# Attention order with two units under way, and a readout with stationary values in column halves

## The chip, the cores and the metric

The kernel runs on one core of one Trainium2 chip. The metric is the device time of one execution in microseconds (us), median over several runs. A core has TensorE (PE, matrix products into PSUM banks), VectorE (DVE), ScalarE (ACT), GpSimd (POOL) and SyncE (SP, which issues most of the DMAs). Each engine works through its own instructions in the order in which the program lists them, and waits where an operand isn't ready or a buffer isn't free.

## The reference

Two layers over 256 tokens of width 1024: a gated DeltaNet, then sparse attention (NSA) with 16 heads of 64 in 4 groups of keys and values, each with a DeepNorm residual and a layer norm. The change lies in the second layer:

```python
proj = x @ w_in                       # q (1024), z (3 x 1024), gate logits (48)
q = rope(q); gates = sigmoid(logits)
p_cmp = masked_softmax(q @ k_cmp.T * scale)   # 15 compressed blocks
p_sel = masked_softmax(q @ k_sel.T * scale)   # all 256 tokens: 4 blocks of 64, top 16
p_win = masked_softmax(q @ k_win.T * scale)   # a window of 512 covers all
o = sum over branches of gates * (p @ v) * silu(z)
y = o @ w_out
x = layer_norm(alpha * x + y)
```

## The kernel before

Tokens lie in two tiles of 128 (t = 0, 1). Projections run as products of three fp32r matmuls (high and low parts of both operands, L233 to L235). Weights stream through a ring of five raw buffers; ACT casts the high part (L181), POOL subtracts the low part (L185). The work of projections is cut into pieces of six matmuls of 512 columns, kept in a list: `fill(n)` puts the next n pieces into PE's order, and runs what was deferred (`step`).

Attention is cut into 24 units. A unit of the first tile holds two heads (keys of the first tile alone), a unit of the second tile one head; a pair of them is read out together. The string `UNITS` gives the order of tiles, `FA` and `FB` the number of fills at two places of each turn of the loop. The steps of a unit:

- `scores` (L1318): four fp32r matmuls into one of two PSUM score buffers.
- `maxima`: DVE adds the mask and takes the negated maxima, for the second tile L1331 to L1334.
- `exps` (L1347, L1348 or L1351, L1352): ACT, into SBUF tiles `pt` (both token branches) and `Pc` (the compressed one).
- `transposes`: PE turns `pt` into the PSUM buffer "t", of which there is one (`ptp`, L1360), and `Pc` (L1362).
- `probs`: ACT copies them to `PT` (L1367) and `PcT` (L1371).
- `readout` (L1386 or L1389, L1392): the turned probabilities are stationary, the values with a 65th column of ones move, into the one PSUM buffer "o". The column of ones gives the denominators.
- `total` (L1400 to L1404), deferred by a step: DVE multiplies by gates, reciprocal denominators and `zz` (silu of z, made at L1218 and L1219), and sums the branches.
- `merge`: four or two column blocks of the sum are turned on PE into buffer "t" (`tp_b`, L1418); ACT makes the high part `x1h` (L1422), DVE the low part `x1l` (L1423), from which the out projection (`pbo` and `pbl`) is computed. There are two merges for the first tile, four for the second.

Behind the out projection stand the residual and layer norm: L905, L906, L912 on DVE, L913 and L914 on POOL, then for the first tile L941 on DVE, L945 on ACT and two products on POOL. In the second half of the out projection the second tile's pieces are 12 matmuls of 256 columns.

Fills of the z projection run out at about 338 us; from there on the pieces are those of the out projection, which need the merges. The main loop computes the scores of unit i first, then copies, fills, reads out unit i-1, and transposes unit i at the end of the same turn.

## Time and profile before

| | us |
|---|---|
| median of 3 runs | 393.89 (393.65 to 393.94) |
| the profiled execution | 393.75 |
| its span | 391.9 |
| PE busy in the span | 379.6 (97%) |
| DVE, ACT, POOL busy | 223.6, 220.6, 246.3 |
| PE busy in the attention stage, 240.9 to 384 | 142.22 of 143.10 |

The span runs from the first instruction to the last; 1.85 us of the profiled execution's time lie outside it. In a timeline a row begins with its start and length in us; matmuls are pipelined, so the spacing of starts tells their pace better than their lengths. An fp32 matmul or transposition leaves one or two records, of which "x8" counts the records. Where an engine was idle before a row, brackets give how long and what ended it.

### The profile page before, as it was taken

To read this page: it belongs to the slowest core of one execution; us is meant where nothing else is said; L and a number is where in the kernel's file an instruction comes from. 1 tells how busy PE (TensorE), PEld (TensorE's weight loads), DVE (VectorE), ACT (ScalarE), POOL (GpSimd) and SP (SyncE) were. 2 spreads that over 40 slices of the span, in tenths; PEclk is the share of its full clock that TensorE was granted. 3 is DMA by queue.
4 is the path that set the end of the run, shared out by engine and by line. 5 is a ranking of instruction groups with operands and counts; after the bars stand their busy time and mean duration, and the time that the engine had idled before them with its cause. 6 is when DMAs were issued, how large, how long until landed. Compare 5 with 4: busy or idle time off the path is not lost.

```text
span 391.9 us, 7551 instructions
## 1 busy us (share of the span) xinstructions
PE 379.6 (97%) x2870; PEld 335.5 (86%) x2870; DVE 223.6 (57%) x591; ACT 220.6 (56%) x433; POOL 246.3 (63%) x154
## 2 busy tenths in 40 slices
PE   8999999999999999999999999999999999999991
PEld 6999999999989987877998788888888888878891
DVE  2868776668623445463641755545656465676726
ACT  4688666656663462625563649566474747456410
POOL 5699999747444846894764988193544637209051
PEclk9999999999999999999999999999999999999997
DMA  7876578654334315573736764243415243301011
GB/s 226 324 223 221 206 232 291 190 135 164 110 110 138 125 35 186 163 248 125 204 118 214 278 223 150 103 153 115 164 39 175 64 153 109 107 3 54 3 54 54
DMA packets 23476, 58.68 MB, mean 150 GB/s; under 512 B 6672, under 2 KB 9232, under 8 KB 23312
## 3 DMA queue, kind: packets, MB, share of 16 engines
q1 hardware_dynamic: 23232, 58.13, 44.9%
q8 instruction: 22, 0.36, 0.4%
q14 instruction: 14, 0.11, 0.1%
q10 hardware_dynamic: 144, 0.07, 0.1%
q0 software_dynamic: 64, 0.01, 0.0%
HBM read 55.96 MB, written 2.23 MB: 148 GB/s over the span
## 4 chain that ended last, share of the span: by engine, by line
PE 42%; DVE 4%; ACT 3%; DMA 2%; POOL 2%; issue 1%; POOLq 0%; DVEq 0%; SPq 0%; ACTq 0%
PE pbz L233 6%; PE pbz L234 6%; PE pbz L235 6%; PE op L1389 4%; PE s L1318 3%; PE ptp L1360 3%; PE op L1392 2%; PE op L1386 1%; DMA raw_bz<-in_bz 1%; ACT hi_bq L181 1%; POOL lo_bq L185 1%; PE pskv L235 1%; PE pbo L233 1%; PE pskv L233 1%; PE pskv L234 1%; PE qtp L1205 1%
## 5 line engine op out<-in xcount | busy, mean ns | idle before, releaser
L185 POOL TENSOR_TENSOR lo_bz<-raw_bz,hi_bz 128x1024 fp32r<-128x1024 f32 x24 | 56.8, 2387 | 39.3 <-ACT hi_bz L181 21.7
L185 POOL TENSOR_TENSOR lo_wqkv<-raw_wqkv,hi_wqkv 128x1024 fp32r<-128x1024 f32 x22 | 52.6, 2408 | 6.7 <-ACT hi_wqkv L181 4.5
L233 PE MATMUL pbz<-hi_bz,x1h 128*128 128x512 f32 x96 | 38.9, 405 | 0.0
L234 PE MATMUL pbz<-hi_bz,x1l 128*128 128x512 f32 x96 | 37.7, 393 | 0.0
L235 PE MATMUL pbz<-lo_bz,x1h 128*128 128x512 f32 x96 | 37.6, 392 | 0.0
L185 POOL TENSOR_TENSOR lo_bo<-raw_bo,hi_bo 128x1024 fp32r<-128x1024 f32 x8 | 18.9, 2390 | 22.8 <-ACT hi_bo L181 17.7
L185 POOL TENSOR_TENSOR lo_skv<-raw_skv,hi_skv 128x1024 fp32r<-128x1024 f32 x12 | 28.4, 2399 | 5.0 <-PE pskv L235 5.0
L185 POOL TENSOR_TENSOR lo_wz<-raw_wz,hi_wz 128x1024 fp32r<-128x1024 f32 x8 | 19.4, 2440 | 16.9 <-ACT hi_wz L181 16.8
L1367 ACT COPY PT<-ptp 128x512 f32<-128x512 f32 x24 | 14.1, 588 | 24.0 <-PE ptp L1360 24.0
L181 ACT CAST hi_bz<-raw_bz 128x1024 fp32r<-128x1024 f32 x24 | 25.2, 1052 | 2.9 <-DMA raw_bz<-in_bz 1.6
L185 POOL TENSOR_TENSOR lo_wo<-raw_wo,hi_wo 128x1024 fp32r<-128x1024 f32 x8 | 18.9, 2385 | 11.5 <-ACT hi_wo L181 11.5
L185 POOL TENSOR_TENSOR lo_bq<-raw_bq,hi_bq 128x1024 fp32r<-128x1024 f32 x8 | 19.1, 2394 | 10.8 <-ACT hi_bq L181 10.8
L181 ACT CAST hi_wqkv<-raw_wqkv 128x1024 fp32r<-128x1024 f32 x22 | 22.7, 1043 | 1.0 <-DMA raw_wqkv<-in_wqkv 1.0
L233 PEld LDWEIGHTS pbz<-hi_bz,x1h 128*128 128x128 f32 x96 | 18.0, 188 | 4.1
L235 PEld LDWEIGHTS pbz<-lo_bz,x1h 128*128 128x128 f32 x96 | 18.0, 188 | 4.1
L234 PEld LDWEIGHTS pbz<-hi_bz,x1l 128*128 128x128 f32 x96 | 18.0, 188 | 2.7
L1351 ACT ACTIVATE pt<-s,mx 128x256 f32<-128x256 f32 x32 | 13.4, 472 | 11.0 <-DVE mx L1334 8.8
L215 PE MATMUL pk<-xh,hi_wqkv 128*128 128x256 f32 x64 | 18.7, 291 | 0.0
L215 PE MATMUL pq<-xh,hi_wqkv 128*128 128x256 f32 x64 | 18.5, 289 | 0.0
L217 PE MATMUL pq<-xh,lo_wqkv 128*128 128x256 f32 x64 | 18.1, 283 | 0.0
L216 PE MATMUL pk<-xl,hi_wqkv 128*128 128x256 f32 x64 | 18.1, 283 | 0.0
L217 PE MATMUL pk<-xh,lo_wqkv 128*128 128x256 f32 x64 | 18.1, 283 | 0.0
(360 smaller groups left out, 1256.1 us busy)
## 6 DMA issues: line engine op xcount, KB each, us to landing
raw_bz<-in_bz SPq DMA_DIRECT2D x24, 512.0 KB, 3.3
raw_wqkv<-in_wqkv SPq DMA_DIRECT2D x23, 512.0 KB, 4.5
raw_skv<-in_skv SPq DMA_DIRECT2D x12, 512.0 KB, 3.3
raw_wz<-in_wz SPq DMA_DIRECT2D x8, 512.0 KB, 3.4
raw_wo<-in_wo SPq DMA_DIRECT2D x8, 512.0 KB, 3.3
raw_bq<-in_bq SPq DMA_DIRECT2D x8, 512.0 KB, 3.7
raw_bo<-in_bo SPq DMA_DIRECT2D x8, 512.0 KB, 3.3
raw_w<-in_w SPq DMA_DIRECT2D x4, 512.0 KB, 3.4
```

Source lines behind the costliest of these rows:

```text
L181: S.copy(h, r)
L185: e.tensor_tensor(l, r, h.bitcast(F32), op=ALU.subtract)
L215: PE.matmul(ps[:, 0:T], wh[:, kt, :], ah[:, kt, :], start=kt == 0, stop=False)
L216: PE.matmul(ps[:, 0:T], wh[:, kt, :], al_[:, kt, :], start=False, stop=False)
L217: PE.matmul(ps[:, 0:T], wl[:, kt, :], ah[:, kt, :], start=False, stop=kt == 7)
L233: PE.matmul(ps, ah[:, kt, tt], wh[:, k4, cols], start=kt == 0, stop=False)
L234: PE.matmul(ps, al_[:, kt, tt], wh[:, k4, cols], start=False, stop=False)
L235: PE.matmul(ps, ah[:, kt, tt], wl[:, k4, cols], start=False, stop=kt == 7)
L1318: PE.matmul(sp[:, j, 0:n], lq, kk[:, hh // 4, c0:c0 + n], start=i == 0, stop=i == 1)
L1351: S.activation(pt[:, :, b, :], s4[:, :, b, :], AF.Exp, bias=mx[:, b:b + 1])
L1367: S.copy(PT.rearrange("p a b c -> p (a b c)"), TP[u])
L1389: PE.matmul(o3[:, r, 1 + b, :], PT[:, j, b, :], vt_[:, b, j, g_, :], start=j == 0, stop=j == 1)
```

## The change

**Order.** Unit i+1 is begun (scores and maxima) in the turn in which unit i-1 is read out, so that two units are under way; its exps stand at the end of that turn, ahead of the transposes of unit i. The eight units of the first tile are moved forward and all stand in the first twelve places. Merges stand directly behind the scores of unit i+1, and `FA` and `FB` are new: two fills behind the copies in the first 14 turns, one later; one behind the scores up to turn 12, then in turns 14, 16 and 18 alone.

**Readout.** The values (128x64, without a column of ones) are stationary and the turned probabilities move, 128 columns; the two token branches go to the two halves of 64 columns of the array, and so to partitions 0 to 63 and 64 to 127 of buffer "t" (`ot`). DVE copies them to SBUF (`oS`, 128x256). A later `turn_back` turns them on PE into buffer "o" (two transposes), adds the compressed branch (L1396 of the kernel after) and runs the total at once. `turn` runs what is waiting to be turned back.

**Denominators.** The exps write the sums of their rows (`accum_out`) into `den`, and the reciprocal reads these. The columns of ones, the small POOL instructions that filled them and one buffer of the tag "ra" are gone.

```diff
@@ -35,9 +35,9 @@
 FIRST = (1, 2)
-UNITS = "001010101101101101111111"
-FA = "3113111011210212044211123"
-FB = "0211121311122110212111000"
+UNITS = "001100101000111111111111"
+FA = "2222222222222211111111111"
+FB = "1111111111111010101000000"
 PRE, TAIL = 4, 2
 NEG = -1e30
...
-    vt_ = wk.tile([P, 2, 2, 4, 65], F32, name="vtok", bufs=1)
-    for a in range(2):
-        for t in range(2):
-            G.memset(vt_[:, a, t, :, 64:65], 1.0)
+    vt_ = wk.tile([P, 2, 2, 4, 64], F32, name="vtok", bufs=1)
-        S.copy(vt_[:, kind, t, :, 0:64], ps[:, 256:512].rearrange("p (a d) -> p a d", d=64))
+        S.copy(vt_[:, kind, t, :, :], ps[:, 256:512].rearrange("p (a d) -> p a d", d=64))
...
             PC[t, h] = wk.tile([P, 2, 16], F32, tag="Pc", name=f"Pc{t}{h}", bufs=4)
-        Pc = PC[t, h - h % 2]
+            DEN[t, h] = sm.tile([P, 2, 3], F32, tag="den", name=f"den{t}{h}", bufs=6)
+        Pc, den = PC[t, h - h % 2], DEN[t, h - h % 2]
         if t == 0:
             for j in range(2):
                 for b in range(2):
-                    S.activation(pt[:, j, b, :], s4[:, j, b, :], AF.Exp, bias=mx[:, 2 * j + b:2 * j + b + 1])
-                S.activation(Pc[:, j, :], sp[:, j, 256:272], AF.Exp, bias=mx[:, 4 + j:5 + j])
+                    S.activation(pt[:, j, b, :], s4[:, j, b, :], AF.Exp, bias=mx[:, 2 * j + b:2 * j + b + 1],
+                                 accum_out=den[:, j, 1 + b:2 + b])
+                S.activation(Pc[:, j, :], sp[:, j, 256:272], AF.Exp, bias=mx[:, 4 + j:5 + j], accum_out=den[:, j, 0:1])
         else:
             for b in range(2):
-                S.activation(pt[:, :, b, :], s4[:, :, b, :], AF.Exp, bias=mx[:, b:b + 1])
-            S.activation(Pc[:, h % 2, :], sp[:, 0, 256:272], AF.Exp, bias=mx[:, 4:5])
+                S.activation(pt[:, :, b, :], s4[:, :, b, :], AF.Exp, bias=mx[:, b:b + 1],
+                             accum_out=den[:, h % 2, 1 + b:2 + b])
+            S.activation(Pc[:, h % 2, :], sp[:, 0, 256:272], AF.Exp, bias=mx[:, 4:5], accum_out=den[:, h % 2, 0:1])
     def transposes(u):
         t, h = u
@@ -1363,48 +1362,52 @@
     def probs(u):
         t, h = u
-        PT = PTT[u] = wk.tile([P, 2, 2, P], F32, tag="ra", name=f"PT{t}{h}", bufs=6)
+        PT = PTT[u] = wk.tile([P, 2, 2, P], F32, tag="ra", name=f"PT{t}{h}", bufs=5)
         S.copy(PT.rearrange("p a b c -> p (a b c)"), TP[u])
         if t == 0 or h % 2:
             h -= h % 2 * t
-            PCT[t, h] = wk.tile([32, P], F32, tag="PcT", name=f"PcT{t}{h}", bufs=2)
+            PCT[t, h] = wk.tile([32, P], F32, tag="PcT", name=f"PcT{t}{h}", bufs=3)
             S.copy(PCT[t, h], S_[u][0:32, 1, 272:400])
-    OP, summed = {}, set()
-    def readout(t, h, half=None):
+    summed = set()
+    backs = []
+    def readout(t, h):
         g_ = h // 4
-        if half != 1:
-            need_z(t, (h + 2) * 192)
-            OP[t] = obank(f"op{t}{h}")
-        o3 = OP[t][:, 0:390].rearrange("p (r b d) -> p r b d", r=2, b=3)
-        for r in range(2) if half is None else (half,):
+        tb = tbank(f"ot{t}{h}")
+        for r in range(2):
             PT = PTT[0, h] if t == 0 else PTT[1, h + r]
-            for b in range(2):
-                if t == 0:
-                    PE.matmul(o3[:, r, 1 + b, :], PT[:, r, b, :], vt_[:, b, 0, g_, :], start=True, stop=True)
-                else:
-                    for j in range(2):
-                        PE.matmul(o3[:, r, 1 + b, :], PT[:, j, b, :], vt_[:, b, j, g_, :], start=j == 0, stop=j == 1)
-        if half == 0:
-            return
-        PE.matmul(o3[:, :, 0, :], PCT[t, h], vbd[:, g_, :, :], start=True, stop=True)
+            for j in range(1 + t):
+                for b in range(2):
+                    PE.matmul(tb[64 * b:64 * b + 64, r * P:(r + 1) * P], vt_[:, b, j, g_, :], PT[:, j if t else r, b, :],
+                              start=j == 0, stop=j == t)
+        oS = wk.tile([P, 2, P], F32, tag="oS", name=f"oS{t}{h}", bufs=2)
+        V.tensor_copy(oS.rearrange("p a b -> p (a b)"), tb[:, 0:2 * P])
+        backs.append(lambda: turn_back(t, h, oS))
+    def turn_back(t, h, oS):
+        need_z(t, (h + 2) * 192)
+        op = obank(f"op{t}{h}")
+        o3 = op[:, 0:384].rearrange("p (r b d) -> p r b d", r=2, b=3)
+        for r in range(2):
+            PE.transpose(op[:, r * 192 + 64:r * 192 + 192], oS[:, r, :], ident)
+        PE.matmul(o3[:, :, 0, :], PCT[t, h], vbd[:, h // 4, :, :], start=True, stop=True)
         rc = sm.tile([P, 2, 3], F32, tag="rc", name=f"rc{t}{h}")
-        o4 = o3[:, :, :, 0:64]
         o_ = zview(t, h * 192, 128).rearrange("p (r d) -> p r d", r=2)
+        rd = op[:, 384:390].rearrange("p (r b) -> p r b", r=2)
         def total():
-            V.reciprocal(o3[:, :, :, 64], o3[:, :, :, 64])
-            V.tensor_tensor(rc, o3[:, :, :, 64], gt[:, t, h * 3:h * 3 + 6].rearrange("p (r b) -> p r b", b=3), op=ALU.mult)
-            V.tensor_tensor(o4, o4, zview(t, h * 192, 384).rearrange("p (r b d) -> p r b d", r=2, b=3), op=ALU.mult)
-            V.tensor_tensor(o4, o4, rc[:, :, :, None].to_broadcast([P, 2, 3, 64]), op=ALU.mult)
-            V.tensor_reduce(o_, o4.rearrange("p r b d -> p r d b"), axis=AX.X, op=ALU.add)
+            V.reciprocal(rd, DEN[t, h])
+            V.tensor_tensor(rc, rd, gt[:, t, h * 3:h * 3 + 6].rearrange("p (r b) -> p r b", b=3), op=ALU.mult)
+            V.tensor_tensor(o3, o3, zview(t, h * 192, 384).rearrange("p (r b d) -> p r b d", r=2, b=3), op=ALU.mult)
+            V.tensor_tensor(o3, o3, rc[:, :, :, None].to_broadcast([P, 2, 3, 64]), op=ALU.mult)
+            V.tensor_reduce(o_, o3.rearrange("p r b d -> p r d b"), axis=AX.X, op=ALU.add)
             summed.add((t, h))
-        defer(1, total)
+        total()
     bT = x1h, x1l
...
@@ -1412,6 +1415,7 @@
     def merge(t, k0, n, nb):
         while not all((t, 2 * k) in summed for k in range(k0, k0 + n)):
+            turn()
             step()
         tp = nb(f"tp_b{t}{k0}")
         for k in range(n):
...
@@ -1473,46 +1477,54 @@
         if g_ == 3:
             add_bo(1, [(1, g_)])
+    def turn():
+        while backs:
+            backs.pop(0)()
     n = len(units)
+    def begin(u):
+        scores(u)
+        maxima(u)
+    begin(units[0])
+    fill(1)
+    exps(units[0])
     for i in range(n + 1):
-        if i < n:
-            scores(units[i])
-        first = i < n and units[i][0] == 0 and not merges
-        if first:
-            maxima(units[i])
         if i:
             probs(units[i - 1])
         step()
-        if i < n and not first:
-            maxima(units[i])
-        fill(int(FA[i]))
-        advance()
+        merge_ = merges.pop(0) if merges else None
+        fill(int(FA[i]) - (i == 0))
         presplit()
-        if i < n:
-            exps(units[i])
         if i:
             t, h = units[i - 1]
-            if t == 0:
-                readout(t, h)
-                if h == 14:
-                    cnt["t0"] = 1
-                    merges += [lambda: merge0(0), lambda: merge0(1)] + ready
-            else:
-                if (units[i - 2] if h % 2 else units[i]) == (1, h ^ 1):
-                    readout(t, h - h % 2, h % 2)
-                elif h % 2:
-                    readout(t, h - 1)
-                if h % 4 == 3:
-                    (merges if cnt["t0"] else ready).append(lambda g_=h // 4: merge1(g_))
+            if t == 0 or h % 2:
+                turn()
+                readout(t, h - h % 2 * t)
+            if (t, h) == (0, 14):
+                cnt["t0"] = 1
+                merges += [lambda: merge0(0), lambda: merge0(1)] + ready
+            if t and h % 4 == 3:
+                (merges if cnt["t0"] else ready).append(lambda g_=h // 4: merge1(g_))
+        if i + 1 < n:
+            begin(units[i + 1])
+        if merge_:
+            merge_()
         fill(int(FB[i]))
+        if i < n:
+            turn()
+        if i + 1 < n:
+            exps(units[i + 1])
         if i < n:
             transposes(units[i])
     while len(merges) > 1:
         advance()
         fill(1)
     add_bo(1, [(1, g_) for g_ in range(3)])
+    fill(1)
+    turn()
     fill(TAIL)
     while merges or fills:
         advance()
```

How the order of instructions moves, at the places that matter below. On PE, at the third merge of the second tile: before, from the end of a fill (`pbo`) over the merge (`tp_b`) and the readout (`op`) to the next unit's transposition (`ptp`) and scores (`s`):

```order
L235 MATMUL pbo_4314<-lo_bo_4230,x1h 128x512
L1418 MATMUL tp_b_4351<-ident,zz_3812 128x128 x2
L1389 MATMUL op_4306<-vtok,PT_4332 128x65 x4
L1392 MATMUL op_4306<-vbd,PcT_4334 128x2x65
L1360 MATMUL ptp_4367<-ident,pt_4356 128x128 x4
L1318 MATMUL s_4372<-kh,qT_2691 128x272
L1318 MATMUL s_4372<-kl,qT_2691 128x272
L1318 MATMUL s_4372<-kh,qT_2691 128x256
L1318 MATMUL s_4372<-kl,qT_2691 128x256
```

and in the changed kernel, from the end of a fill (`pbl`):

```order
L235 MATMUL pbl_4431<-lo_bo_3941,x1h 128x256
L1314 MATMUL s_4444<-kh,qT_2686 128x272
L1314 MATMUL s_4444<-kl,qT_2686 128x272
L1314 MATMUL s_4444<-kh,qT_2686 128x256
L1314 MATMUL s_4444<-kl,qT_2686 128x256
L1422 MATMUL tp_b_4454<-ident,zz_3850 128x128 x2
L1359 MATMUL ptp_4465<-ident,pt_4407 128x128 x4
L1361 MATMUL s_4387<-ident,Pc_4355 32x128
L233 MATMUL pbl_4430<-hi_bo_3952,x1h 128x256
```

The readout that stood between `tp_b` and `ptp` is gone from there, the scores have come ahead of `tp_b`, and `ptp` follows it directly; both write buffer "t".

On DVE, up to the low part `x1l` of that merge, before:

```order
L905 SCALAR_TENSOR_TENSOR x_2042<-x_2042,pbo_4198 128x512
L906 BN_STATS st_blw_4311<-x_2042 128x6
L1331 TENSOR_TENSOR s_4327<-s_4327,cb 128x256
L1332 TENSOR_TENSOR s_4327<-s_4327,cb 128x16
L1333 TENSOR_REDUCE mx_4336<-s_4327 128x2
L1334 TENSOR_REDUCE mx_4336<-s_4327 128x1
L1423 TENSOR_TENSOR x1l<-tp_b_4351,x1h 128x2x128
```

and in the changed kernel, from the end of a total:

```order
L1406 TENSOR_TENSOR op_4397<-op_4397,rc_4401 128x384
L1407 TENSOR_REDUCE zz_3850<-op_4397 128x128
L905 SCALAR_TENSOR_TENSOR x_2042<-x_2042,pbo_4279 128x512
L906 BN_STATS st_blw_4276<-x_2042 128x6
L912 BN_AGGR mv_blw_4420<-st_blw_4276 128x2
L941 SCALAR_TENSOR_TENSOR nb_blw_4424<-mv_blw_4420 128x1
L1327 TENSOR_TENSOR s_4444<-s_4444,cb 128x256
L1328 TENSOR_TENSOR s_4444<-s_4444,cb 128x16
L1329 TENSOR_REDUCE mx_4449<-s_4444 128x2
L1330 TENSOR_REDUCE mx_4449<-s_4444 128x1
L1427 TENSOR_TENSOR x1l<-tp_b_4454,x1h 128x2x128
```

The second half of the first tile's layer norm (L905 to L941) and the end of a total now stand ahead of the maxima (L1327 to L1330) and of `x1l`; before, only the first half of it did.

On ACT, near the end of the units, before (exps, then the copies of the same unit):

```order
L1351 ACTIVATE pt_4356<-s_4327,mx_4336 128x2x128 x2
L1352 ACTIVATE Pc_4357<-s_4327,mx_4336 128x16
L1367 COPY PT_4377<-ptp_4367 128x512
L1351 ACTIVATE pt_4401<-s_4372,mx_4384 128x2x128 x2
L1352 ACTIVATE Pc_4357<-s_4372,mx_4384 128x16
L1367 COPY PT_4416<-ptp_4410 128x512
L1371 COPY PcT_4418<-s_4372 32x128
```

and in the changed kernel:

```order
L1349 ACTIVATE pt_4522,den_4461<-s_4502,mx_4507 128x2x128 x2
L1351 ACTIVATE Pc_4460,den_4461<-s_4502,mx_4507 128x16
L1366 COPY PT_4531<-ptp_4526 128x512
L1366 COPY PT_4551<-ptp_4545 128x512
L1370 COPY PcT_4553<-s_4502 32x128
```

Before, the copy `PT` that follows a unit's exps is that of the same unit; now it is that of the unit before, and the next unit's exps stand ahead of it.

## Rows read from the trace of the kernel before

**Rows 1.** busy time by stretch: length, busy us (instructions) by engine, PEclk, DMA.
```profile
240.90:337.88 96.98, 96.98 (x552) 82.77 (x552) 54.79 (x129) 58.62 (x135) 52.62 (x23) 1.00 0.38 129
337.88:349.83 11.95, 11.07 (x78) 9.23 (x76) 9.98 (x25) 6.30 (x17) 0.00 (x0) 1.00 0.02 5
```

**Rows 2.** PE timeline, two readouts and what follows: start, length, engine, line.
```profile
248.03 1.00 PE L1386 MATMUL op<-vtok,PT 128*128 128x65 f32 x8
248.96 0.48 PE L1392 MATMUL op<-vbd,PcT 32*128 32x130 f32 x2
249.38 0.50 PE L233 MATMUL pbz<-hi_bz,x1h 128*128 128x512 f32 x1
249.72 0.40 PE L234 MATMUL pbz<-hi_bz,x1l 128*128 128x512 f32 x1
249.96 0.40 PE L235 MATMUL pbz<-lo_bz,x1h 128*128 128x512 f32 x1
...
272.99 1.89 PE L1389 MATMUL op<-vtok,PT 128*128 128x65 f32 x16
```

**Rows 3.** the same view, 342 to 349 us, where the merges begin.
```profile
342.50 0.38 PE L1318 MATMUL s<-kh,qT 128*128 128x272 f32 x1
...
342.95 0.28 PE L1318 MATMUL s<-kl,qT 128*128 128x256 f32 x1
343.37 0.66 PE L1418 MATMUL tp_b<-ident,zz 128*128 128x128 f32 x4
344.21 2.00 PE L1389 MATMUL op<-vtok,PT 128*128 128x65 f32 x16 [0.19 <-DVE zz L1404]
...
348.91 1.11 PE L1389 MATMUL op<-vtok,PT 128*128 128x65 f32 x8 [0.37 <-DVE zz L1404]
```

**Rows 4.** DVE timeline beside it: a total's first step, first maxima, x1l.
```profile
341.96 0.20 DVE L1400 RECIPROCAL op<-op 128x6 f32<-128x6 f32 x1
...
344.07 0.42 DVE L1331 TENSOR_TENSOR s<-s,cb 128x256 f32<-128x256 f32 x1
...
345.44 0.68 DVE L1423 TENSOR_TENSOR x1l<-tp_b,x1h 128x512 fp32r<-128x512 f32 x1
```

**Rows 5.** PE timeline at the compression, which alternates between two column halves.
```profile
208.12 0.39 PE L235 MATMUL pbq<-lo_bq,x1h 128*128 128x512 f32 x1
208.44 1.97 PE L1133 MATMUL hpT<-raw_w,C 128*61 128x128 f32 x32
210.33 0.50 PE L233 MATMUL pbq<-hi_bq,x1h 128*128 128x512 f32 x1
```

**Rows 6.** groups on ACT, 240 to 384: busy us, mean ns, idle before.
```profile
L1367 ACT COPY PT<-ptp 128x512 f32<-128x512 f32 x24 | 14.1, 588 | 24.0 <-PE ptp L1360 24.0
L1351 ACT ACTIVATE pt<-s,mx 128x256 f32<-128x256 f32 x32 | 13.4, 472 | 11.0 <-DVE mx L1334 8.8 <-DVE op L1400 2.2
L1347 ACT ACTIVATE pt<-s,mx 128x128 f32<-128x128 f32 x32 | 10.1, 377 | 8.3 <-DVE mx L1329 6.7 <-DVE op L1400 1.6
...
L1352 ACT ACTIVATE Pc<-s,mx 128x16 f32<-128x16 f32 x16 | 4.4, 278 | 0.0
L1371 ACT COPY PcT<-s 32x128 f32<-32x128 f32 x16 | 4.0, 250 | 0.0
...
L1422 ACT CAST x1h<-tp_b 128x256 fp32r<-128x256 f32 x4 | 1.5, 373 | 8.2 <-PE tp_b L1418 8.2
```

**Rows 7.** the same view for DVE.
```profile
L1423 DVE TENSOR_TENSOR x1l<-tp_b,x1h 128x256 fp32r<-128x256 f32 x4 | 1.7, 425 | 3.1 <-ACT x1h L1422 3.1
```

**Rows 8.** DVE timeline at the first tile's layer norm.
```profile
369.48 0.69 DVE L905 SCALAR_TENSOR_TENSOR x<-x,pbo 128x512 f32<-128x512 f32 x1 [0.25 <-PE pbo L235]
...
372.14 0.16 DVE L941 SCALAR_TENSOR_TENSOR nb_blw<-mv_blw 128x1 f32<-128x1 f32 x1 [1.00 <-POOL mv_blw L914]
```

**Rows 9.** durations of one line's second instruction: min/median/max ns.
```profile
L499 DVE DVE_READ_ACCUMULATOR2_ANT ssk<- x16: 82/83/86, 35.9 to 59.4; 128x1 f32 x16
```

**Rows 10.** as rows 1, one microsecond behind the last matmul.
```profile
386.00:387.00 1.00, 0.00 (x0) 0.00 (x0) 0.91 (x2) 0.00 (x0) 0.92 (x2) 0.94 0.00 0
```

More of the change, by code (lines that the diff above doesn't have):

```diff
@@ L1025, in rope @@
         A = s3
-        B = wk.tile([P, n, 64], F32, tag="ra", name=f"rb{name}", bufs=6)
+        B = wk.tile([P, n, 64], F32, tag="ra", name=f"rb{name}", bufs=5)
         V.tensor_tensor(B[:, :, 0:32], s3[:, :, 32:64], si[:, None, 0:32].to_broadcast([P, n, 32]), op=ALU.mult)
@@ L1094, in trunk @@
     G.memset(hid, 0.0)
-    vbd = wk.tile([32, 4, 2, 65], F32, name="vbd", bufs=1)
+    vbd = wk.tile([32, 4, 2, 64], F32, name="vbd", bufs=1)
     bd = cb[0:32, C_BD:C_BD + 2]
-    G.tensor_copy(vbd[:, :, :, 64], bd[:, None, :].to_broadcast([32, 4, 2]))
     fill(2)
@@ L1185, in place @@
             for g_ in range(4):
-                V.tensor_tensor(vbd[:, g_, :, 0:64], vcp[0:32, None, g_ * 64:(g_ + 1) * 64].to_broadcast([32, 2, 64]),
+                V.tensor_tensor(vbd[:, g_, :, :], vcp[0:32, None, g_ * 64:(g_ + 1) * 64].to_broadcast([32, 2, 64]),
                                 bd[:, :, None].to_broadcast([32, 2, 64]), op=ALU.mult)
@@ L1216, in bz_done @@
         zdone.add((c, t))
-        th = wk.tile([P, 512], F32, tag="ra", name=f"th{c}{t}", bufs=6)
+        th = wk.tile([P, 512], F32, tag="ra", name=f"th{c}{t}", bufs=5)
         S.activation(th, ps, AF.Tanh, scale=0.5)
@@ L1305, in trunk @@
     units = [order0.pop(0) if k == "0" else order1.pop(0) for k in UNITS]
-    S_, PT_, PTT, PC, PCT, MX, TP = {}, {}, {}, {}, {}, {}, {}
+    S_, PT_, PTT, PC, PCT, MX, TP, DEN = {}, {}, {}, {}, {}, {}, {}, {}
     cnt = {"n": 0}
```

## The prediction

> **What bounds the kernel now.** I began with the busy time by stretch [rows 1]. The program's last stage, attention, runs from 240.9 us to about 384. In its long first part TensorE (PE) is busy for all of 96.98 us; in the 12 us behind it, where the projections have run out and the merges begin, for 11.07 of 11.95. So time is lost or won only by shorter PE work or by PE waiting, and DVE and ACT count only where PE waits for them. Next came the PE timeline of a readout [rows 2], and that of the stretch with gaps [rows 3]: tp_b follows the last score matmul by 0.42 us where the scores themselves follow one another by 0.1 to 0.2, the readout behind it starts 0.84 after tp_b's start though its four records should take 0.46 by the pace in [rows 2], and 348.91 shows another wait for DVE's total. By the busy column the gaps are 0.9 us, by the starts (a few more of the same kind) 1.9; I take 1.5. That is all the waiting the change can remove. Last I read DVE and ACT in that stretch [rows 4, 6], since the new order makes PE wait for them more directly.
>
> **PE work removed.** A first-tile readout today is four fp32 matmuls, eight records, 0.93 us from start to the compressed matmul L1392, so 0.23 a matmul, with L1392 0.42 behind it [rows 2]. A second-tile pair has eight matmuls, 1.89 us. The new form sends each product to one half of the array's columns. Its nearest row is the compression L1133, whose fp32 matmuls also alternate between two column halves: 32 records, 16 matmuls, 1.89 us, 0.118 each, entered 0.32 us after the matmul before it where 0.23 is that one's pace [rows 5], so 0.09 for the entry. A first-tile readout becomes 4 x 0.118 + 0.09 = 0.56, plus two transposes back, a record of 0.11 each, = 0.78: it saves 0.15. A pair becomes 0.94 + 0.09 + 0.22 = 1.25 against 1.83: it saves 0.58. The compressed matmul stays, and so does the slow first matmul behind an fp32 block (0.34 rather than 0.23). Eight of each: 1.2 + 4.6 = **5.8 us saved**. Bounds: 7.2 without the entries (16 x 0.09), and a loss of 5 if the halves do not pair (then 0.23 a matmul as today, and 0.31 more for each of 16).
>
> The rows show an entry of 0.09 us into column halves. The Trainium skill, "TensorEngine Tiling (Array Packing)", Key Properties, says that changing the tiling mode drains TensorE, which speaks against doing so 16 times for 4 or 8 matmuls; without the entries the sum below would be 401.6, with the drain as large as the measured entry it is 403.0, and no run here shows one that is larger.
>
> **What the new order makes PE wait for.** The first third of the order is sound: with a fill before and one behind each unit's scores, PE has 4.7 us or more of work between a unit's scores and the first use of its probabilities, and the chain there (maxima 1.65, exps 4 x 0.38 + 2 x 0.29, copy 0.59 [rows 6]; the maxima from three rows like those of rows 4) is about 4.4. The margin is thin, so I put 1.5 us on it (0 to 4), with the hi casts of ring weights that now queue behind those copies on ACT.
>
> Units are counted from 0. From unit 13 on the fill behind the scores (FB) is 0 wherever a merge stands. There PE goes scores, tp_b, ptp with nothing between, and ptp needs the one PSUM buffer "t" that tp_b fills, so it waits until DVE has made x1l. DVE has the next unit's maxima queued ahead of x1l, and these cannot start before the scores end. The kernel before has the same queue on DVE (344.07 to 345.44, 1.37 us, then x1l 0.68 [rows 4]), but a readout of 16 records covers it [rows 3]. Handoffs between engines I put at 0.15 in all. Each wait follows:
> - first merge (16 rows of x1l, 512 wide): 1.37 + 0.68 + 0.15 - 0.42 = 1.8;
> - third merge: the unit before was turned back, and its total (341.96 to 344.07, 2.1) and the L1219 product (0.69) stand ahead of the maxima: 2.1 + 0.69 + 1.37 + 0.43 [rows 7] + 0.25 = 4.85, while PE has ptp 0.44, a fill of six at 0.23 = 1.4, scores 0.5, tp_b 0.22 = 2.5: 2.35. The second merge has its fill and costs nothing;
> - fourth merge, without L1219: 1.7;
> - fifth (the second tile's third): now also layer norm's L905, L906, L912, two steps on POOL and L941, 369.48 to 372.30, 2.8 us [rows 8], all ahead of the maxima: 2.1 + 2.8 + 1.37 + 0.43 + 0.4 = 7.1 against 2.45: **4.65**. In the kernel before the same chain stands behind the maxima, where nobody waits for it;
> - from unit 19 FB is 0 throughout, and on ACT the exps of the next unit stand ahead of the copy PT of this one, so that the readout (or the next ptp, by the same buffer) waits for maxima 1.37, exps 2 x 0.42 + 0.28, PT 0.59: 3.15 against ptp and a fill, 1.8: 1.35; three units later against turn-back, ptp and a fill: 0.65; and the very last readout comes right behind its ptp, a bare copy: 0.7;
> - the last tp_b is followed by products that need it, where before an independent unit of 12 matmuls stood: x1h 0.37, x1l 0.43, handoffs 0.2 [rows 6, 7]: 1.0.
>
> Sum 1.8 + 2.35 + 1.7 + 4.65 + 1.35 + 0.65 + 0.7 + 1.0 = **14.2 us**. These are sums of durations that are in the trace; what they lack is chance overlap, so I bound them by 9 and 17.
>
> **Other pieces.** The sixteen copies oS (128x256) on DVE, about 0.42 us each by the equally wide L1331 [rows 4], have a fill or scores beside them on PE, except one, 0.1; with no such cover 0.4 each. The reciprocal now reads the exps' sums, same size. The total runs at once after the turn-back rather than a step later, which is why it meets the maxima above. The dropped columns of ones and five small POOL instructions are worth nothing beside PE at 100% [rows 1]. The sums: no ACT instruction of before has an accumulator. On DVE one such operation has a second instruction of 83 ns that reads it back [rows 9]. The smallest ACT instruction is 0.25 [rows 6]. So a sum costs 0 to 0.28; I take 0.13, nearer the DVE row. Three exps a unit stand in three ACT waits above and partly in the merges: **0.8 us**; those of the first third are in the 1.5.
>
> **Sum.** The profiled run took 393.75 us, span 391.9 and 1.85 around it; the median is 393.89, so no correction. 393.75 - 5.8 - 1.5 + 14.2 + 1.5 + 0.8 = 402.95, said as **403.0 us**. The tail behind the last matmul (384 to 391.9) keeps its instructions.
>
> **Rivals.**
> - *Faster.* The mechanism is DVE's backlog at the merges: if the totals and the layer norm are done by the time the scores land, only maxima and x1l are left, four waits of 1.6, and the ACT waits are covered. Then 393.75 - 7.2 - 1.9 + 6.4 = 391.1. It decides as soon as the new waits together stay under some 7.3. For it: DVE is busy for only 54.79 of 96.98 us earlier. Against: it has 9.98 of 11.95 where merges stand [rows 1], and the order itself puts the totals ahead. 0.09.
> - *Small waits:* the new ones at their lower bound, 9 in all, and the first third at 0 to 2.5: 396.3 to 399. 0.15.
> - *Sums dear:* each a whole small ACT instruction, 0.28; some 0.15 more on 60 exps of the first third, whose margin is used up, and twice the 0.8: 403 + 2 + 0.9 = 406. 0.18.
> - *Clock.* The granted clock is 1.00 (the 2.4 GHz level) throughout the stage [rows 1], and 0.94 from 386 to 387, where PE has been idle since 384 [rows 10], so it fell there. The kernel before has no wait of a us in the stage; the 4.65 would be the first inside it. If the 1.2 GHz level is granted there, the matmuls from it to the next wait (a fill 1.4, a readout 1.03, scores 0.5, turn-back and ptp 0.66: 3.6) take up to twice as long: up to +3.6; with half to all of it, 405 to 407. The Trainium skill, "TensorE: Matmul & The Clock Gate", Part 1, says that an idle engine is throttled to that level and full rate comes back only after sustained work; no row here shows such a fall inside the span. 0.2.
> - *Halves don't pair:* 403 + 5.8 + 5 = 414. Against it stands L1133's pace. 0.03.
>
> **How the numbers follow.** The forecast as worked out, 399 to 405, has 0.35. The range leaves out the faster case below 396.5, and the halves that don't pair, and ends where clock and dear sums meet: 396.5 to 408.5. A measurement of this kernel can tell 0.2%, 0.8 us, from no change: faster (under 393.1) 0.09, same 0.03, slower 0.88.
>
> **What would show it.** In the changed kernel's PE timeline: ot eight records in about 0.5 us and the pair 16 in about 0.95; PE busy less by about 6 us in the stage; at each merge but one a gap before ptp with DVE's x1l as releaser, the longest 4 to 5 us with L941 and the maxima ahead on DVE; gaps before ot with PT as releaser near the end; the granted clock in the us after the long gap. I am wrong if PE is still busy throughout the last 40 us, if ot takes 0.23 a matmul, or if the first third of the stage shows gaps of several us.

## The result

The changed kernel takes 418.88 us (418.08 to 419.82, 4 runs) against 393.77 before: a ratio of 1.063, with an interval from 1.0605 to 1.065. It is slower, as forecast, but by 25 us instead of 9; the time lies 10 us above the range. The profiled execution took 418.96 us, its span 417.2.

The first view is the list of what PE waited for, from 175 us on (total, number of waits, the longest):

```profile
PE ptp L1359 <- DVE x1l L1427: 7.5, 4, 2.2
PE s L1314 <- DVE gt L1293: 4.2, 1, 4.2
PE pbl L233 <- DVE x L905: 2.3, 1, 2.3
PE ktp L1058 <- DVE x1l L962: 2.3, 1, 2.3
PE ot L1384 <- ACT PT L1366: 2.1, 2, 1.5
PE ptp L1359 <- ACT PT L1366: 0.8, 1, 0.8
PE pskv L235 <- POOL lo_skv L185: 0.7, 1, 0.7
PE qtp L1201 <- DVE kl L1168: 0.7, 1, 0.7
PE pbl L233 <- ACT x1h L1426: 0.5, 1, 0.5
```

The first, third, fifth, sixth and last rows, all after 343 us, are what the prediction had counted. Two small ones of 0.7 (`pskv`, `qtp`) lie ahead of the attention stage. The second (`s` waiting for the gates `gt`, 4.2 us) and the fourth (`ktp` waiting for `x1l`, 2.3 us) are not in it. The fourth isn't in the attention stage at all: the first scores start at 246.98 us, where they started at 240.90 before, so 6.1 us are lost ahead of anything that the prediction looked at. The busy time by stretch, which answers to [rows 1] (length, busy us and instructions of PE, PE's weight loads, DVE, ACT and POOL, then the granted clock, the DMA share and GB/s):

```profile
246.98:260.00 13.02, 8.82 (x39) 7.08 (x39) 5.16 (x11) 7.98 (x31) 5.31 (x3) 0.87 0.43 150
260.00:340.00 80.00, 80.00 (x466) 62.54 (x465) 45.99 (x109) 48.44 (x153) 42.70 (x19) 1.00 0.33 111
340.00:410.50 70.50, 56.20 (x396) 45.85 (x394) 39.89 (x101) 29.88 (x97) 19.97 (x12) 0.98 0.12 40
```

The middle is full, as it was before; PE now stands for 4.2 of the first 13 us and for 14.3 of the last 70.5.

**The loss ahead of attention.** It is a load. These are the rows of SP's timeline in the changed kernel (start, length; a row with a count is a run of loads, its length the time over which they were issued):

```profile
150.63 23.11 SPq L161 DMA_DIRECT2D raw_skv<-in_skv  x8
173.83 0.38 SPq L1007 DMA_DIRECT2D cb<-in_cb  x1
```

The same rows of the kernel before:

```profile
149.70 16.09 SPq L161 DMA_DIRECT2D raw_skv<-in_skv  x6
165.88 0.38 SPq L1007 DMA_DIRECT2D cb<-in_cb  x1
```

`cb`, the constants with sines and masks, was issued behind six loads of ring weights in these rows before and is now issued behind eight; three more loads of `raw_skv` came behind it before, one does now. Each of these waits until POOL has freed a ring buffer, so `cb` leaves SP 8 us later. DVE needs it for the first rotary product (L1027); queued behind that is L962, which reads the PSUM buffer that PE's next transposition (`ktp`) fills. DVE's timeline of the changed kernel; the bracket is the idle time ahead of a row and what ended it:

```profile
178.50 0.29 DVE L1027 TENSOR_TENSOR rbk<-pskv,cb 128x128 f32<-128x128 f32 x1 [8.04 <-DMA cb<-in_cb]
...
180.85 1.29 DVE L962 TENSOR_TENSOR x1l<-tp_x1h,x1h 128x512 fp32r<-128x512 f32 x2
```

PE's timeline beside it:

```profile
181.59 1.12 PE L1058 MATMUL ktp<-ident,hlk 128*128 128x128 f32 x4 [2.27 <-DVE x1l L962]
182.36 0.78 PE L233 MATMUL pskv<-hi_skv,x1h 128*128 128x512 f32 x1
182.94 0.63 PE L234 MATMUL pskv<-hi_skv,x1l 128*128 128x512 f32 x1
183.36 0.63 PE L235 MATMUL pskv<-lo_skv,x1h 128*128 128x512 f32 x1
```

And the busy time of that stretch, the granted clock third from the end:

```profile
180.00:185.00 5.00, 3.41 (x10) 2.91 (x11) 3.82 (x9) 2.93 (x7) 0.00 (x0) 0.54 0.26 95
```

PE waits 2.27 us, and the matmuls behind that start 0.43 us apart instead of 0.23, up to 187.2: the granted clock of the stretch is 0.54, the 1.2 GHz level. From 181.59 to 187.47 PE does in 5.9 us what takes 3.2 at the pace behind it. The wait of 2.27 and these 2.7 are most of the 6.1 us. In the kernel before the clock is 1.00 there.

**The first turn of the loop.** The second unit's scores need the score buffer in which the gates' logits lie. ACT's timeline, from a table load over the first of the exps to the gates' exp:

```profile
249.42 1.28 ACT L1344 ACT_TABLE_LOAD   x1 [1.02 <-DVE mx L1325]
250.71 0.37 ACT L1344 ACTIVATE pt<-s,mx 128x128 f32<-128x128 f32 x1
250.98 0.19 ACT L1344 ACTIVATION_READ_ACCUMULATOR pt<-s,mx 128x1 f32 x1
251.07 0.36 ACT L1344 ACTIVATE pt<-s,mx 128x128 f32<-128x128 f32 x1
...
252.60 0.27 ACT L1288 ACTIVATE gq<-gq 128x96 f32<-128x96 f32 x1
```

DVE's timeline, the first and the last of the gates' steps:

```profile
252.90 0.27 DVE L1289 TENSOR_SCALAR gq<-gq 128x96 f32<-128x96 f32 x1 [3.59 <-ACT gq L1288]
...
254.30 0.24 DVE L1293 TENSOR_SCALAR gt<-gq,cb 128x16 f32<-128x16 f32 x1
```

PE's timeline, on either side of the wait:

```profile
250.10 0.39 PE L235 MATMUL pbz<-lo_bz,x1h 128*128 128x512 f32 x1
254.69 0.36 PE L1314 MATMUL s<-kh,qT 128*128 128x272 f32 x1 [4.20 <-DVE gt L1293]
```

On ACT the gates' exp (L1288) comes behind all six exps of the first unit, each with an instruction that reads its sum back; DVE then needs 252.90 to 254.5 for the gates, and PE starts at 254.69. That is 4.4 us over the usual pace. The table load that the first exp brings with it, 1.28 us, is a part of that: in the kernel before it stands ahead of the gates' exp, at 241.40 us, where ACT does it while DVE still works on the first maxima; now it begins only when these maxima are there. Behind the wait the clock falls again (granted 0.57 from 255 to 259), for some 1.6 us of loss.

**The readout.** PE's timeline in the changed kernel, a first-tile readout (`ot`) and its turning back (`op`):

```profile
261.31 0.39 PE L235 MATMUL pbz<-lo_bz,x1h 128*128 128x512 f32 x1
261.63 0.66 PE L1384 MATMUL ot<-PT,vtok 128*64 128x128 f32 x8
262.22 0.39 PE L1314 MATMUL s<-kh,qT 128*128 128x272 f32 x1
262.45 0.29 PE L1314 MATMUL s<-kl,qT 128*128 128x272 f32 x1
...
264.20 0.38 PE L1395 MATMUL op<-ident,oS 128*128 128x128 f32 x2
264.51 0.48 PE L1396 MATMUL op<-vbd,PcT 32*128 32x128 f32 x2
264.93 0.66 PE L1359 MATMUL ptp<-ident,pt 128*128 128x128 f32 x4
```

The same view, a second-tile pair:

```profile
347.60 1.09 PE L1384 MATMUL ot<-PT,vtok 128*64 128x128 f32 x16
348.62 0.40 PE L1314 MATMUL s<-kh,qT 128*128 128x272 f32 x1
```

The new readout takes 0.59 us where [rows 2] have 0.93, the pair 1.02 where they have 1.83; two transposes back 0.31. It is entered 0.32 behind the last product, and the first scores behind it take 0.23 where 0.13 is the pace.

**The late waits.** DVE's timeline around the fifth merge:

```profile
385.05 0.56 DVE L1407 TENSOR_REDUCE zz<-op 128x128 f32<-128x384 f32 x1
385.53 0.68 DVE L905 SCALAR_TENSOR_TENSOR x<-x,pbo 128x512 f32<-128x512 f32 x1
...
388.18 0.16 DVE L941 SCALAR_TENSOR_TENSOR nb_blw<-mv_blw 128x1 f32<-128x1 f32 x1 [1.00 <-POOL mv_blw L914]
388.26 0.43 DVE L1327 TENSOR_TENSOR s<-s,cb 128x256 f32<-128x256 f32 x1
...
389.63 0.41 DVE L1427 TENSOR_TENSOR x1l<-tp_b,x1h 128x256 fp32r<-128x256 f32 x1
```

PE's timeline in the same stretch:

```profile
386.26 0.39 PE L233 MATMUL pbl<-hi_bo,x1h 128*128 128x256 f32 x1 [2.30 <-DVE x L905]
...
387.56 0.38 PE L1422 MATMUL tp_b<-ident,zz 128*128 128x128 f32 x2
390.10 0.66 PE L1359 MATMUL ptp<-ident,pt 128*128 128x128 f32 x4 [2.15 <-DVE x1l L1427]
```

L905 of the layer norm runs directly behind a total (to 385.53), L941 ends at 388.3, and only then come the maxima and `x1l`: the chain of the prediction, at the length that it gave (385.53 to 388.26, 2.7 us). PE waits for it in two places instead of one: 2.3 us for L905, since the next product (`pbl`) needs the PSUM buffer that L905 reads, and 2.15 us at `ptp`, with a fill and `tp_b` between them.

### The profile page after: what moved, and what is told of

Same layout as the page of the kernel before. It is cut to its first block, busy times and chain, and to the rows that moved or that the text cites. A ratio compares the mean times of both kernels' runs of the same rounds, so it can differ in the third digit from the quotient of the medians.

```text
span 417.2 us, 7704 instructions
## 1 busy us (share of the span) xinstructions
PE 385.3 (92%) x2902; PEld 330.2 (79%) x2902; DVE 229.3 (55%) x607; ACT 227.5 (55%) x529; POOL 246.2 (59%) x149
## 4 chain that ended last, share of the span: by engine, by line
PE 38%; DVE 8%; ACT 5%; DMA 3%; POOL 2%; issue 1%; POOLq 0%; DVEq 0%; SPq 0%; ACTq 0%
PE pbz L235 5%; PE pbz L233 5%; PE pbz L234 5%; PE s L1314 3%; PE ot L1384 3%; PE ptp L1359 3%; DMA raw_bz<-in_bz 1%; PE op L1396 1%; ACT hi_bq L181 1%; DVE mx L1329 1%; POOL lo_bq L185 1%; DMA cb<-in_cb 1%; PE pskv L233 1%; PE pskv L234 1%; PE pskv L235 1%
## 5 line engine op out<-in xcount | busy, mean ns | idle before, releaser
L1349 ACT ACTIVATE pt<-s,mx 128x256 f32<-128x256 f32 x32 | 14.9, 471 | 28.4 <-PE op L1395 11.6
L1387 DVE COPY oS<-ot 128x256 f32<-128x256 f32 x16 | 6.8, 424 | 36.1 <-PE ot L1384 36.1
L1359 PE MATMUL ptp<-ident,pt 128*128 128x128 f32 x96 | 16.0, 290 | 8.2 <-DVE x1l L1427 7.5
L1344 ACT ACTIVATE pt<-s,mx 128x128 f32<-128x128 f32 x32 | 11.5, 370 | 19.7 <-DVE mx L1325 19.7
L913 POOL TENSOR_SCALAR mv_blw<-mv_blw 128x1 f32<-128x1 f32 x2 | 1.0, 502 | 34.3 <-DVE mv_blw L912 34.3
L1359 PEld LDWEIGHTS ptp<-ident,pt 128*128 128x128 f32 x96 | 10.7, 144 | 11.8 <-DVE x1l L1427 8.4
L1314 PE MATMUL s<-kh,qT 128*128 128x272 f32 (+1 forms) x48 | 14.7, 326 | 4.2 <-DVE gt L1293 4.2
```

Of the source, the lines that this page charges most:

```text
L1314: PE.matmul(sp[:, j, 0:n], lq, kk[:, hh // 4, c0:c0 + n], start=i == 0, stop=i == 1)
L1344: S.activation(pt[:, j, b, :], s4[:, j, b, :], AF.Exp, bias=mx[:, 2 * j + b:2 * j + b + 1], accum_out=den[:, j, 1 + b:2 + b])
L1349: S.activation(pt[:, :, b, :], s4[:, :, b, :], AF.Exp, bias=mx[:, b:b + 1], accum_out=den[:, h % 2, 1 + b:2 + b])
L1359: PE.transpose(tp[:, (2 * j + b) * P:(2 * j + b + 1) * P], pt[:, j, b, :], ident)
L1387: V.tensor_copy(oS.rearrange("p a b -> p (a b)"), tb[:, 0:2 * P])
```

## The experiments

| kernel | us, median (lowest to highest) | ratio to before, interval |
|---|---|---|
| changed | 418.88 (418.08 to 419.82) | 1.0627 (1.0605 to 1.065) |
| e1_cb: cb early, by memsets | 414.33 (413.9 to 415.4) | 1.0526 (1.05 to 1.0552) |
| e11_cb_act: cb on ACT's queue | 413.42 (412.73 to 414.09) | 1.0496 (1.0481 to 1.0512) |
| e2_gates: gates ahead of the exps | 412.59 (410.09 to 412.88) | 1.0463 (1.0427 to 1.05) |
| e3_cb_gates: e1 and e2 | 409.1 (408.17 to 411.54) | 1.0399 (1.0357 to 1.044) |
| e4_merge_o: e3, merges in o | 404.64 (404.41 to 405.21) | 1.0279 (1.0254 to 1.0304) |
| e5_exps: e3, exps behind copies | 408.31 (406.87 to 410.29) | 1.0378 (1.0341 to 1.0414) |
| e6_merge_exps: e4 and e5 | 398.75 (397.73 to 400.16) | 1.0134 (1.0107 to 1.0161) |
| e9_norm: e6, layer norm moved | 395.64 (395.14 to 396.19) | 1.005 (1.0033 to 1.0066) |
| e10_cover: e9, two fills moved | 396.07 (395.38 to 397.34) | 1.006 (1.0039 to 1.008) |
| e12_same_half: e9, halves not alternating | 395.87 (395.79 to 396.14) | 1.0052 (1.0036 to 1.0069) |
| e13_best: e9, three small moves | 398.33 (396.44 to 399.18) | 1.0104 (1.008 to 1.0128) |
| e7_sums: before with the exps' sums | 394.65 (394.07 to 395.52) | 1.0021 (1.0007 to 1.0035) |
| e8_halves: before's order, new readout | 407.16 (406.28 to 410.17) | 1.0371 (1.0324 to 1.0417) |

**Is it cb?** The theory: `cb` is late because of its place on SP. The rival: the smaller tiles and the moved memory slow that stretch, and `cb` is late with it. The first kernel puts four memsets back on POOL:

```diff
     vt_ = wk.tile([P, 2, 2, 4, 64], F32, name="vtok", bufs=1)
+    for a in range(2):
+        for t in range(2):
+            G.memset(vt_[:, a, t, :, 63:64], 1.0)
```

> The changed kernel with four 0.2 us memsets of vtok put back on GpSimd; they write a column that a later copy overwrites. With them the load of the constants cb stands on SP's queue where it stood before the change, ahead of two ring loads. If cb's late arrival is what costs the time ahead of attention, the first scores come 6.1 us earlier (at 240.9 instead of 247.0), no clock below 1.00 is left between 180 and 190 us, and the time is 418.9 - 6.1 = 412.8. Rival: the smaller tiles and the shifted memory make that stretch slower and cb only comes late with it: 418.9 within 0.8.

Measured: 414.33, 4.5 less. `cb` is issued at 166.28 us, the clock is 1.00 from 180 to 185, and the first scores start at 240.93, so the 6.1 us are back at that point; some 1.5 of them are lost again later, where the granted clock falls in three stretches of attention (0.90 from 250 to 260, 0.69 from 352 to 356, 0.79 from 383 to 391) instead of two (0.57 from 255 to 259, 0.50 from 358 to 361). The memsets do it by moving no work worth speaking of: with them the built program has `cb` ahead of the two loads on SP, without them behind. A second kernel gets there by another road, leaving the memsets out:

```diff
-    nc.sync.dma_start(cb, I["cb"])
+    nc.scalar.dma_start(cb, I["cb"])
```

> The changed kernel with the one load of the constants cb issued from ACT's queue instead of SP's, and no memsets. If it is the place behind two ring loads on SP that delays cb, the time is that of the kernel with the memsets: 414.3 within 1. Rival: the memsets did something else, and the time stays at 418.9.

Measured: 413.42, `cb` issued at 165.19 us and the first scores at 240.57. Two unlike edits that bring `cb` back to its time, and the ring loads with it, give nearly the same time, so the rival falls. Why four memsets on POOL decide where a load stands on SP is not shown.

**The gates.**

```diff
-    defer(2, gates)
+    defer(1, gates)
```

> The changed kernel with the gates deferred by one step instead of two, so that their instructions stand ahead of the first unit's exps on ACT and DVE. If the second unit's scores wait for the gates because these stand behind six exps, the wait of 4.2 us shrinks to 0.5 to 1.3 and the 1.7 us of half clock behind it goes: 418.9 - 3.1 - 1.7 = 414.1, or 413.0 at best. Rival: the wait is for the first unit's own exps or for a buffer, and moves: 418.9 within 0.8.

Measured: 412.59, and PE's wait there is 0.5 us. The gain of 6.3 is more than the wait with the half clock behind it (4.4 - 0.5 + 1.6 = 5.5). Not all of it is from the gates: in its profile the first scores start at 245.18 us instead of 246.98, though `cb` is as late as before (173.19). The clock behind the late `cb` fell for a shorter time (granted 0.72 from 180 to 185 us and 0.94 from 185 to 190, where the changed kernel has 0.54 and 0.77). From the first scores to the last product pass 157.6 us instead of 162.1, so the gates gave 4.5. Both edits together:

> Both edits. If the two losses are independent, their sum: 418.9 - 6.1 - 5.2 = 407.6, and what is left over the kernel before, some 14 us, lies in the last 65 us of attention as the prediction had it. Rival: the early gain is given back by later waits for weights, since everything then comes earlier: above 410.

Measured: 409.1, 9.8 less than the changed kernel, and 1.0 short of the two gains added, of which e2's held 1.8 that are not from the gates. In its profile the transposes of the last queries wait 1.8 us for DVE at 225 us, which no other of these kernels does for that long; the runs of this kernel spread over 3.4 us, and that share stays open. What is left over before, 15 us, lies where the prediction put it.

**What PE waits for late.** Theory A: for `x1l` behind the maxima, through the buffer "t" that the merge and the next transposes share. Theory B: for the copy `PT` behind the next unit's exps. One kernel takes A away, by giving the merges the buffer "o":

```diff
-        merge(0, 4 * q, 4, tbank)
+        merge(0, 4 * q, 4, obank)
...
-        merge(1, 2 * g_, 2, tbank)
+        merge(1, 2 * g_, 2, obank)
```

> Both edits, and the merges turn into PSUM buffer o instead of t, so that the next transposes no longer wait for the low part x1l. Theory A, x1l behind the maxima is the whole of the four waits of 1.86, 2.06, 1.90 and 2.32 us: about 8 less than with both edits alone, 399.5. Theory B, the copy PT stands behind the next unit's exps, which stand behind the same maxima, so that the readout waits instead: only 1 to 3 less, 405 to 406.5.

What PE waited for in it, the largest rows:

```profile
PE ot L1387 <- ACT PT L1369: 7.1, 7, 1.5
PE pbl L233 <- DVE x L905: 2.3, 1, 2.3
```

Measured: 404.64. The waits for `x1l` (7.5 us) are gone, and those of the readout for `PT` have grown from 2.9 us in e3 to 7.1. The other takes B away alone:

```diff
         if i:
             probs(units[i - 1])
+            if i < n:
+                exps(units[i])
...
-        if i + 1 < n:
-            exps(units[i + 1])
         if i < n:
             transposes(units[i])
```

> cb and gates mended as before (409.1), merges in buffer t, and the exps of the next unit put behind the copies PT and PcT of this one on ACT. If the readouts wait for PT only because exps stand ahead of it, those waits go (1.0 in the first third, 1.7, 0.9 and 0.8 near the end) and the four waits for x1l stay: 405 to 406. Rival: the exps now come too late for the next transposes, which wait in their place: 409 or more.

Measured: 408.31, 0.8 less and within the spread of the two; the waits for `x1l` stay at 7.7 us, and the granted clock is 0.65 from 370 to 380 us, so that a part of the gain is lost there. With both edits:

> cb and gates mended, merges in buffer o, and the exps behind the copies. If the two queues (x1l behind the maxima on DVE for buffer t, PT behind the exps on ACT) are the two wakes of one stall, each alone gives 3 to 4.5 and both together some 12: 397, with the wait for L905 (2.5) left. Rival: a third wait, DVE's backlog of totals and layer norm, takes over: 401 to 404.

Measured: 398.75, 10.4 less than e3 where the two alone give 4.5 and 0.8: they are one stall with two releasers, and each theory had half of it. A part of each gain over e3 is e3's own wait at 225 us, which is 0.4 us at most in the profiles of the three: from the first scores to the last product pass 156.2 us in the profile of e3, 154.5 in e4, 158.0 in e5 (some 3 of it for the fall of the clock) and 148.4 in e6, so that 7.8 of the 10.4 are in the stage. What PE still waits for, the two largest rows:

```profile
PE pbl L233 <- DVE x L905: 2.3, 1, 2.3
PE ot L1387 <- ACT PT L1369: 0.6, 1, 0.6
```

Of theory B's waits 0.6 us are left, of theory A's 0.4 (a turning back for `x1l`).

**The layer norm.** L905 and L906 come directly behind their product, and L941 a step later:

```diff
-            defer(1, lambda: done(512 * c, pb_[t, c]))
+            done(512 * c, pb_[t, c])
...
-        V.scalar_tensor_tensor(nb, mv[:, 0:1], -1.0, mv[:, 1:2], op0=ALU.mult, op1=ALU.mult)
         def half(c):
+            if c == 0:
+                V.scalar_tensor_tensor(nb, mv[:, 0:1], -1.0, mv[:, 1:2], op0=ALU.mult, op1=ALU.mult)
```

> As the kernel with both queues mended (398.75), and the first tile's layer norm moved on DVE: L905 and L906 come directly behind the product that they read, ahead of oS and the total, and the small L941 product a step later, so that it doesn't hold the queue while GpSimd works. If PE's wait of 2.47 us before pbl is for L905 behind the total, it goes, and with it the half clock behind it (1 to 1.5 us): 395.0 to 396.3. Rival: oS comes later by L905 and L906 (1.4) and PE waits there instead: 397.5 to 399.

Measured: 395.64. The busy time of the 8 us in question, in e6 without the edit:

```profile
364.00:372.00 8.00, 5.69 (x35) 5.42 (x34) 6.03 (x16) 3.74 (x12) 2.27 (x4) 0.79 0.01 2
```

The same stretch in e9:

```profile
364.00:372.00 8.00, 7.80 (x69) 6.97 (x69) 5.65 (x17) 5.32 (x18) 4.13 (x4) 1.00 0.10 35
```

PE is busy for 7.80 of 8 us instead of 5.69, and the clock is 1.00 instead of 0.79. The wait is worth 2.5 us and the clock up to 8 x 0.21 = 1.7; the gain is 3.1, so up to 1 us came back; the small waits that e9 has for `oS` (0.3) and behind L941 (0.2) are half of that.

**What is left.** Two kernels cover the small waits of e9. The first moves a fill ahead of the second unit's scores (`FA` begins with 3) and the second half's pieces one turn earlier. The second has the same fill, taken from turn 3, the second merge in "t" again, and both halves of the layer norm's end two steps later.

> As the kernel before it in this list, with one more fill ahead of the second unit's scores and the pieces of the out projection's second half put on the list one turn earlier, so that the last readout no longer comes right behind its transposes. Two waits of 0.7 and 0.8 us go: 393.6 to 395, level with the kernel before the change. With no wait left but the last merge's, the gain of the readout in column halves (some 4 us of PE) should show and does not if its entries and the turning back cost more than the rows say: then above 396.

> As the same kernel (395.64), with a third fill ahead of the second unit's scores (one less at turn 3), the second merge back in buffer t, and the layer norm's last DVE and ACT steps two steps later. Waits of 0.7, 0.8 and 0.2 us go: 394.0, level with the kernel before. If the new readout is worth the 4.0 us of its own rows, this should come out at 392 or less, since its waits then are 2 us more than those of before; if entries into the column halves and the slow matmuls behind them eat half of it, at 394.

Measured: 396.07 and 398.33. Each removed wait came back as another: with e10 PE waits 1.1 us for POOL's low parts, which now fall behind the faster use of weights, and 0.8 us for the last total, and in its profile (397.34 us) the clock falls behind the latter (granted 0.51 from 384.5 to 388); with e13 a `ptp` waits 1.1 us for its exps, because the products that stood between it and the `ptp` ahead of it in e9 are used up, and two merges wait 0.6 us each, for a total and for L944 (0.2 in e9; the step that is L941 in the changed kernel). Neither reaches the kernel before.

**Do the halves need to alternate?**

```diff
-            for j in range(1 + t):
-                for b in range(2):
+            for b in range(2):
+                for j in range(1 + t):
```

> As the kernel with both queues mended and the layer norm moved (395.64), but the readout's matmuls are ordered so that in a second-tile pair two of one column half follow each other before two of the other half. If the pace of 0.118 us a matmul comes from alternating between halves, a pair's readout goes from 1.02 to some 1.4 to 1.9 us and the time to 398.5 to 402. Rival: each half runs at that pace by itself, since 64 stationary columns are what makes it short: 395.6 within 0.8, readouts unchanged.

Measured: 395.87, the same; a pair takes 1.07 us instead of 1.02. The pace of 0.12 us a matmul doesn't come from alternating with every matmul; no run keeps a whole readout in one half.

**The parts by themselves, in the kernel before.** The sums alone: in `exps` as in the changed kernel, and the reciprocal reads `DEN` instead of the column of ones, which still moves through the readout.

> The kernel before with the exps' sums as denominators and nothing else changed (the ones still move through the readout, their result is not used). About 0.1 us more on each of 96 exps on ACT, which has idle time before it almost everywhere: the same, 393.8 within 0.8. Rival: every unit's chain from scores to transposes is longer by 0.3 to 0.6 and PE waits for some of them: 395 to 397.

Measured: 394.65, a ratio of 1.0021 (1.0007 to 1.0035): 0.8 us, at the edge of the forecast. And the new readout with the old order, the sums included:

> The order of the kernel before (its UNITS, FA, FB, and its places of scores, exps and merges) with the new readout: stationary values in column halves, turned back at the end of the turn, denominators from the sums; odd and even heads of the second tile are read out together. In the changed kernel's trace the readouts with their turning back take 18.0 us against 22.05: 389.7 if nothing waits. Rival: the next transposes wait for the copy oS, which holds buffer t, for some 0.2 to 0.5 us each: 392 to 396.

What PE waited for in it, the two largest rows:

```profile
PE op L1398 <- DVE oS L1390: 4.4, 5, 1.7
PE ot L1387 <- DVE x1l L1430: 4.2, 3, 2.3
```

Measured: 407.16. The rival's mechanism is right and its price far too small: the turning back waits 4.4 us for `oS`, which DVE makes behind totals, maxima and the product with `z`, and the readout 4.2 us for `x1l` in buffer "t", which merge, readout and transposes now share; behind the longest of these waits, 2.3 us, the granted clock is 0.50 from 352 to 358 us. The old order has no room for a readout that goes through DVE. No run has the new order with the old readout, so what the order costs by itself is known only from the waits above.

## Why the prediction was wrong

**The direction and the late waits were right.** The prediction summed them to 14.2; by the starts of PE's rows they are 1.86, 2.06, 1.90, 1.71, 2.46 + 2.32, 0.91, 0.81 and 0.62: 14.65. No term is off by more than 0.4. The experiments change one thing in it: each was priced as one queue, but in several of these places a second queue ends not much earlier (of the 7.5 us of waits for `x1l`, 4.2 came back at the readout in e4), so the price of a wait was right and what its removal gives was not in it.

**The step that failed** is the sentence that the five small POOL instructions are worth nothing. As work they are; but the order of SP's loads is not the order in which the code calls them, and it changed with them (with four of the five, the memsets, put back, it is the old one). The prediction looked for moved instructions on PE, DVE and ACT in the attention stage, and nowhere on SP. What changed on SP is two rows of ring loads ahead of `cb`. Price 6.1 us, of which e1 gives back 4.5 and e11 5.5.

**The second** is that the first third of the order is sound. From the third unit on it is: PE is busy for 20.00 of each 20 us from 260 to 340 us, and the 1.5 us set aside were not needed. But the first turn was never walked through. The exps of the first unit are put ahead of the loop, and with them and the table load ahead of the gates, on whose buffer the second scores wait: 4.4 us, and 1.6 of half clock. The prediction itself had named gaps of several us in the first third as a sign that it is wrong.

**The third** is a term that was mis-sized, the saving of 5.8. The rows of readout and turning back, without the entries, were to save 7.2 and save 4.0 (18.0 us of e9's stage, against 22.05 before): a readout takes 0.59 and 1.02 where its matmuls at 0.118 are 0.47 and 0.94, and a pair of transposes 0.31 where 0.22 was taken. The entries into column halves are as priced, 0.10 each and 1.6 in all. Some 0.5 more goes to slow first matmuls behind the additional fp32 blocks. Over the whole stage, less its waits by the starts, PE needs 140.0 us in e9 (240.18 to 385.27, less 5.05) and 141.3 before (240.90 to 383.77, less 1.6): **1.2 us** are left of 5.8 (0.9 with the 1.9 that the prediction read for the old waits); by the busy column (141.85 and 141.99) it is 0.1. Of the 0.7 between 1.2 and the terms named, some 0.5 lie in the transposes `ptp`: directly behind the block of `op` they take 0.41 or 0.49 us, behind a product 0.35 or 0.44, and 15 of them stand so in e9, 5 before. The rest stays open. The Trainium skill, "TensorEngine Tiling (Array Packing)", Key Properties, says that changing the mode drains the engine; these rows agree in that the entry costs, and what it costs is the measured 0.10 us each.

**The clock** was among the rivals at the place where the wait was longest. It fell in the changed kernel at 180, 255 and 358 us, behind waits of 2.27, 4.2 and 1.89; at the 4.65, which came as two, it didn't (granted 1.00 from 384 to 391). In other kernels it did fall behind these same two waits, in e1 (granted 0.53 from 385 to 388.5) and in e2 (0.51 from 383.5 to 387); in e3 it fell nowhere in the stage. A fall in the changed kernel cost 1.5 to 2.7 us, within the 3.6 that the rival allowed. The Trainium skill, "TensorE: Matmul & The Clock Gate", Part 1, has the fall behind idle time; these runs agree in that each fall stands behind a wait, and show that a wait of about 2 us may or may not be followed by one.

**Sums.** Each exp has a second instruction of 0.2 us, of which 0.09 shows in the starts (250.98 to 251.07), near the 0.13 taken.

Added up: 393.75 + 6.1 + 4.4 + 14.65 + 1.6 and 1.5 of half clock in the attention stage - 1.2 - 1.6 of old waits = 419.2, against 418.96.

## What to carry to other kernels

Before costing a change, compare every engine's order over the whole program, the queue of loads first: an instruction that is dropped because it costs nothing can let two loads pass the one that everything waits for. Walk the first and the last turn of a loop as well as the middle. Where PE waits, look for the second queue that ends at nearly the same time, since removing one alone can give less than half of the stall (here 4.5 and 0.8 of 10.4, though the 0.8 held a fall of the clock), and count what stands around a new form of matmul, the transposes and the first matmul after it, before its own pace.

## What the runs showed of the hardware

An fp32 matmul with 64 stationary and 128 moving columns took 0.12 us, where the one of before, with 128 stationary and 65 moving, took 0.23 [rows 2]; and it did so whether or not the next goes to the other half: a pair of readouts is 1.02 us alternating and 1.07 with two in a row. ACT's sums are a second instruction, 197 to 216 ns long in the groups by line, but the next exp starts 0.09 us behind its start. And a wait of 2.27 us was followed by 5 us and more of matmuls at half pace, so that it cost about twice its length; behind two waits of 2.30 and 2.15 us in the same kernel the clock stayed at 1.00. The table load ahead of the first exp took ACT 1.28 us, wherever that exp stood.
